# Four plain column tiles instead of three, the norm's matmul inside the first up product, and mixing chunk by chunk, in a two-layer decoder trunk

## The chip, the core and the metric

The kernel runs on one core of a Trainium2 chip. A core has five engines with instruction queues of their own, each worked off in order: TensorE (PE; its weight loads are listed as PEld), VectorE (DVE), ScalarE (ACT), GpSimd (POOL) and SyncE (SP), the last of which issues most DMA transfers here. The metric is the device time of one execution in microseconds, as the median of several.

## What is computed

Sixteen learned meta tokens stand ahead of 512 real ones, so L = 528; the model width is D = 1024. Two pre-norm residual layers follow, each a token mixer and a SwiGLU feed-forward (D_FF = 2816), and a last RMSNorm. Everything is float32.

```python
def rmsnorm(x, g):
    y = xf * lax.rsqrt(jnp.mean(xf * xf, axis=-1, keepdims=True) + EPS)
    return y * g
def swiglu(h, w_gate, w_up, w_down):
    return (jax.nn.silu(h @ w_gate) * (h @ w_up)) @ w_down

h = concatenate([meta, x])                       # (528, 1024)
h = h + pool_mixer(rmsnorm(h, g0), pool_w, pool_scale)   # layer 0: means over 2, 4, 8, 16 tokens, then 256x256 mixing by group
h = h + swiglu(rmsnorm(h, f0), gate0, up0, down0)
h = h + sb_mixer(rmsnorm(h, g1), w_qkv, w_o)             # layer 1: stick-breaking attention, 16 heads
h = h + swiglu(rmsnorm(h, f1), gate1, up1, down1)
return rmsnorm(h, final_norm)[16:]
```

## The kernel before

The residual stream is held transposed, in eight chunks `h` of 128 channels by 528 tokens (`hT[c]`). A float32 product is done as three fp32r products of a high and a low part (`mm3`, L106: high by high, high by low, low by high). The high part of a weight is a cast on ACT (L92, names that end in h), the low part a subtraction on DVE (L97, names that end in l). Raw weights arrive by DMA on SP's queue in six buffers; the split parts have eight buffers each for high and low.

**Layer 0's start.** The pool mixer writes pooled chunks into PSUM and then mixes them: sixteen tiles `mix` of 128 by 264, one for each chunk c and each token half hf, halves outside and chunks inside. DVE adds each to `h` (L266). When both halves of a chunk are done, `norm.chunk(c)` prepares it for the feed-forward: ACT scales it by the norm's gains and rounds it (`f0uh`, L152), DVE forms the rest (`f0ul`, L153), ACT squares it and DVE sums the squares over the chunks (`f0sq`, L161; the last by `add_eps`, L128). The reciprocal root of the mean (`rstd`) isn't needed for these: the products take the unscaled chunks, and the result is scaled on the way out. The matmul by `ones` (L173, output `fb0p`; `fb1p` in layer 1) sums over the partitions and spreads the sum to all of them, and `rstd_of` makes `fb0r` of it: a table function on ACT (L135) and one Newton step on DVE (L136 to L139). PSUM has eight banks: in the mixing all eight are a pool of their own, so the first feed-forward tile gets a bank when the last mix tile has been read.

**The feed-forward** works on 22 column tiles of 128 of D_FF, in six rounds (`ROUNDS`: 2, then 4 each). The first `PLAIN` tiles are plain products: gate, then up, each over eight chunks (`pp`, in two pieces of 264 tokens in layer 0 and in one of 512 in layer 1). The others are done by Strassen's scheme with seven products (`pa`, `pb`, `pc`) instead of eight. These need `operands()`: normed chunks `xn` (which need `fb0r`), their sums `t` and high and low parts `xh`, `xl` (L381, L387, L389, L390) in four sets, and sums `s` of the weights (L400) with splits `ws_0` to `ws_6`. The down products of a round (`pd`; L304 adds them to `h`, layer 1 has them transposed back, L325 and L331) are spread through the next round.

**What sets the order.** The program is written in dependence order; a scheduler with estimated durations sets the order of the instructions on each engine ahead of the run, and the engine keeps to it. `tc.issue_after(ins)` holds the instructions written inside it behind `ins` on the same engine, without a wait. Layer 1 has the same scheme behind the attention, whose output product `pw` DVE adds to `h` (L660) in chunks of 128 by 512.

## Time and profile before

| | |
|---|---|
| median of 3 runs | 1059.41 us (1058.34 to 1059.82) |
| the profiled execution | 1062.8 us |
| its span | 1061.0 us |
| mean granted clock of TensorE | 0.985 |
| busy: PE, PEld, DVE | 1023.1, 949.3, 856.6 us |
| busy: ACT, POOL | 556.9, 6.2 us |
| read from HBM, written | 92.43 MB, 2.10 MB |
| chain that ended last | PE 78%, DVE 17% |

A row of the timeline has the start, the duration, the engine, the line, the operation, output<-inputs by the program's names (buffer numbers left out), the shapes and the count of rows joined; in brackets how long the engine was idle before it, and what ended that. Matmuls overlap in the pipeline, so from start to start tells more than a row's duration; DVE instructions overlap by some 0.08 us as well. A list of waits has the total, the number of times and the longest. A slice of the timeline has its bounds, then busy time and count of each engine, the clock granted to TensorE (1.00 is full), the DMA share and GB/s.

### The profile page before, as it was taken

The numbers are of one execution on the slowest core, as the hardware profiler recorded it, in microseconds if no ns is written. First come the engines' busy times: TensorE is split into PE (matmuls) and PEld (weight loads), VectorE is DVE, ScalarE is ACT, GpSimd is POOL, SyncE is SP. The second block draws the span as 40 slices with busy tenths as digits, with TensorE's granted clock in tenths as the row PEclk, the third lists the DMA queues.
The fourth block names the chain that finished last, engine by engine and source line by source line (L and its number), as shares of the span: only waits on it lengthen the run. The fifth ranks groups of instructions, "written<-read, shape, count | busy, mean of one in ns | idle before, by whom it ended". The sixth has DMA issues, their size and how long they took to land.

```text
span 1061.0 us, 18586 instructions
## 1 busy us (share of the span) xinstructions
PE 1023.1 (96%) x7302; PEld 949.3 (89%) x7302; DVE 856.6 (81%) x1529; ACT 556.9 (52%) x1131; POOL 6.2 (1%) x16
## 2 busy tenths in 40 slices
PE   8998999999999999999999998989999999999997
PEld 6997999999999998998888886867899999999985
DVE  7899987888878777678888987779977877788755
ACT  7555645454444455455555454555655444455544
POOL 1000000000000010000000000000000000000000
PEclk9999999999999999999999998989999999999999
DMA  9212323333333332211111211211223223333302
GB/s 351 72 51 69 128 94 100 101 100 100 100 100 100 99 120 82 78 40 61 40 51 37 69 58 66 80 62 58 100 100 115 84 100 99 100 100 120 109 31 80
DMA packets 43112, 95.73 MB, mean 90 GB/s; under 512 B 3328, under 2 KB 20096, under 8 KB 43024
## 3 DMA queue, kind: packets, MB, share of 16 engines
q1 hardware_dynamic: 42272, 93.40, 26.2%
q8 instruction: 57, 0.93, 0.3%
q10 hardware_dynamic: 752, 1.14, 0.3%
q14 instruction: 31, 0.25, 0.1%
HBM read 92.43 MB, written 2.10 MB: 89 GB/s over the span
## 4 chain that ended last, share of the span: by engine, by line
PE 78%; DVE 17%; issue 2%; ACT 1%; DMA 1%; SPq 0%; ACTq 0%; DVEq 0%
PE pb L106 15%; PE pd L106 11%; PE pd L331 11%; PE pa L106 10%; PE pc L106 10%; PE pj L106 9%; PE pp L106 4%; DVE kp L581 2%; PE pw L106 2%; PE z L567 2%; DVE xl L390 1%; DVE a L619 1%; PE t L594 1%; DVE t L387 1%; DVE sg L583 1%
## 5 line engine op out<-in xcount | busy, mean ns | idle before, releaser
L304 DVE TENSOR_TENSOR h<-pd,h 128x264 f32<-128x264 f32 x96 | 40.9, 427 | 14.0 <-PE pd L106 14.0
L92 ACT CAST ws_3h<-rgate 128x512 fp32r<-128x512 f32 x38 | 23.6, 620 | 53.3 <-PE pb L106 47.8
L581 DVE TENSOR_TENSOR_SCAN kp<-kp,estrip 128x1344 f32<-128x1344 f32 x16 | 47.3, 2954 | 3.8 <-ACT kp L576 3.4
L92 ACT CAST ws_4h<-s 128x512 fp32r<-128x512 f32 x38 | 23.6, 621 | 46.6 <-PE pa L106 27.7
L92 ACT CAST ws_5h<-s 128x512 fp32r<-128x512 f32 x38 | 23.6, 621 | 45.8 <-PE pb L106 34.7
L433 DVE TENSOR_TENSOR u<-pb,m 128x264 f32<-128x264 f32 (+1 forms) x38 | 16.3, 428 | 38.6 <-PE pb L106 38.6
L106 PE MATMUL pa<-xl,ws_0h 128*128 128x264 f32 (+1 forms) x152 | 43.3, 285 | 3.1 <-DVE xl L390 3.0
L106 PE MATMUL pb<-xl,ws_1h 128*128 128x264 f32 (+1 forms) x152 | 43.3, 285 | 1.0 <-DVE xl L390 1.0
L106 PE MATMUL pc<-xl,ws_2h 128*128 128x264 f32 (+1 forms) x152 | 43.1, 283 | 0.9 <-DVE xl L390 0.9
L106 PE MATMUL pb<-xh,ws_1h 128*128 128x264 f32 (+1 forms) x152 | 43.6, 287 | 0.2 <-ACT xh L389 0.2
L106 PE MATMUL pa<-xh,ws_3h 128*128 128x264 f32 (+1 forms) x152 | 43.6, 287 | 0.0
L106 PE MATMUL pa<-xl,ws_3h 128*128 128x264 f32 (+1 forms) x152 | 43.5, 286 | 0.0
L106 PE MATMUL pa<-xh,ws_3l 128*128 128x264 f32 (+1 forms) x152 | 43.3, 285 | 0.0
L106 PE MATMUL pc<-xh,ws_2l 128*128 128x264 f32 (+1 forms) x152 | 43.2, 284 | 0.0
L106 PE MATMUL pa<-xh,ws_0h 128*128 128x264 f32 (+1 forms) x152 | 43.1, 284 | 0.0
L106 PE MATMUL pb<-xh,ws_6l 128*128 128x264 f32 (+1 forms) x152 | 43.0, 283 | 0.0
L106 PE MATMUL pa<-xh,ws_0l 128*128 128x264 f32 (+1 forms) x152 | 43.0, 283 | 0.0
L106 PE MATMUL pb<-xh,ws_4l 128*128 128x264 f32 (+1 forms) x152 | 43.0, 283 | 0.0
L106 PE MATMUL pc<-xl,ws_5h 128*128 128x264 f32 (+1 forms) x152 | 42.9, 283 | 0.0
L106 PE MATMUL pb<-xh,ws_1l 128*128 128x264 f32 (+1 forms) x152 | 42.9, 283 | 0.0
L106 PE MATMUL pb<-xl,ws_4h 128*128 128x264 f32 (+1 forms) x152 | 42.9, 282 | 0.0
L106 PE MATMUL pc<-xh,ws_5h 128*128 128x264 f32 (+1 forms) x152 | 42.9, 282 | 0.0
(1179 smaller groups left out, 4110.9 us busy)
## 6 DMA issues: line engine op xcount, KB each, us to landing
rgate<-in_ffn_w_gate_dram SPq DMA_DIRECT2D x44, 512.0 KB, 3.5
rup<-in_ffn_w_up_dram SPq DMA_DIRECT2D x44, 512.0 KB, 3.5
rd<-in_ffn_w_down_dram SPq DMA_DIRECT2D x42, 512.0 KB, 3.6
rq<-in_sb_w_qkv_dram SPq DMA_DIRECT2D x8, 512.0 KB, 3.5
rk<-in_sb_w_qkv_dram SPq DMA_DIRECT2D x8, 512.0 KB, 3.4
rv<-in_sb_w_qkv_dram SPq DMA_DIRECT2D x8, 512.0 KB, 3.4
rwo<-in_sb_w_o_dram SPq DMA_DIRECT2D x8, 384.0 KB, 3.0
h<-in_x_t_dram SPq DMA_DIRECT2D x8, 264.0 KB, 6.9
```

The source lines that it names most:

```text
L92: nc.scalar.copy(hi, v[:, j:j + w])
L106: last = nc.tensor.matmul(o, lhsT=w, rhs=xx[:, sl], start=start and i == 0, stop=stop and i == 2, skip_group_check=more)
L304: nc.vector.tensor_tensor(out=hv, in0=pd, in1=hv, op=ALU.add)
L331: nc.tensor.matmul(pd, lhsT=hid[j][x_][:, ts], rhs=w_[:, sl], start=r > 0 and i + j == 0, stop=j == len(hid) - 1 and i == 2, skip_group_ch ...
L387: nc.vector.tensor_tensor(out=o, in0=a, in1=b, op=ALU.subtract)
L390: nc.vector.tensor_tensor(out=xl[i][:, m, :], in0=o, in1=f32(xh[i][:, m, :]), op=ALU.subtract)
L433: tt(out=u[:, a], in0=pb, in1=m1, op=ALU.add)
L567: nc.tensor.matmul(tz[:, hd, c:c + k1 - k0], lhsT=qq[hs, i * P:(i + 1) * P], rhs=kk[hs, k0:k1], start=j == 0 and c == 0, stop=False, skip_ ...
L581: nc.vector.tensor_tensor_scan(kp[:, hd, ::-1], kp[:, hd, ::-1], estrip[:, ::-1], 1.0, op0=ALU.mult, op1=ALU.max)
L583: return nc.vector.tensor_tensor(out=sg[:, hd, 0:STRIP - 1], in0=sg[:, hd, 0:STRIP - 1], in1=kp[:, hd, 1:STRIP], op=ALU.mult).ins
L594: nc.tensor.transpose(o, sg[:, c0:c0 + n], ident)
L619: nc.vector.scalar_tensor_tensor(a0[r, i], f32(a0h[r]), lo_rows[r], p2[r, 256:384], op0=ALU.mult, op1=ALU.add)
```

## The change

Six edits go together. (1) `PLAIN` is 4: tile 3 becomes plain in both layers. (2) The mixing runs over chunks outside and halves inside, so that a chunk is complete, and its `norm.chunk` can begin, after every second mix tile. (3) The weight splits of a plain tile behind the first are held back on their engine: in layer 0 those of tiles 1 and 2, in layer 1 those of tile 1, behind `add_eps`'s instruction (`norm.done`); the later ones behind the last instruction of `rstd`. The hold acts on DVE, where both instructions run. (4) The norm's matmul stands inside tile 0's up product, right behind the one for chunk `FB` = 4, and the rest of the product behind it; the up product is held behind the gate product. (5) Gate and up results are read out of PSUM after both products are written. (6) `add_eps` and `norm_bcast` hand on their instructions for this.

```diff
-PLAIN = 3
+PLAIN = 4
+FB = 4
...
             if c == KC - 1:
-                add_eps(self.acc, sq, self.acc)
+                self.done = add_eps(self.acc, sq, self.acc)
...
-                nc.tensor.matmul(p, lhsT=ones, rhs=acc[:, o:o + h], start=i == 0, stop=i == len(accs) - 1)
+                last_bcast[:] = [nc.tensor.matmul(p, lhsT=ones, rhs=acc[:, o:o + h], start=i == 0,
+                                                  stop=i == len(accs) - 1).ins]
...
-        for hf in range(2):
-            for c in range(KC):
+        for c in range(KC):
+            for hf in range(2):
...
             def plain(f):
-                parts = [wsplit(raw_gu(kind, f), f"w{kind}{f}") for kind in ("gate", "up")]
+                parts = []
+                for kind in ("gate", "up"):
+                    with tc.issue_after(norm.done if f <= 2 - layer else fst[1]) if f else nullcontext():
+                        parts.append(wsplit(raw_gu(kind, f), f"w{kind}{f}"))
                 g, sg, u = (gw(f"{i}{f}") for i in ("g", "sg", "u"))
-                for dst, (wh, wl) in zip((g, u), parts):
+                prods = []
+                for i, (dst, (wh, wl)) in enumerate(zip((g, u), parts)):
                     pts = [ps(f"pp{f}", "w")[:, :sl.stop - sl.start] for sl in pieces]
+                    prods.append((dst, pts))
+                    mark = last if i and not fst else None
                     for k in range(KC):
-                        mm3([(t, slice(t0 + sl.start, t0 + sl.stop)) for t, sl in zip(pts, pieces)], wh[k], wl[k],
-                            uh[k], ul[k], k == 0, k == KC - 1)
-                    if not fst:
-                        fst.extend((norm_bcast([acc], f"fb{layer}", "d"), last_rstd[0]))
+                        with tc.issue_after(mark) if mark else nullcontext():
+                            last = mm3([(t, slice(t0 + sl.start, t0 + sl.stop)) for t, sl in zip(pts, pieces)], wh[k],
+                                       wl[k], uh[k], ul[k], k == 0, k == KC - 1)
+                        if i == 1 and k == FB and not fst:
+                            with tc.issue_after(last):
+                                fst.extend((norm_bcast([acc], f"fb{layer}", "d"), last_rstd[0]))
+                            mark = last_bcast[0]
+                for dst, pts in prods:
                     for t, sl in zip(pts, pieces):
```

How the edits move instructions is shown at three places; the numbers in the names tell buffers apart. Lines of the changed kernel are two to thirteen higher than those of the same statement before. First, DVE in layer 0 around the last residual add of the mixing, before:

```order
L97 TENSOR_TENSOR wgate1l_816<-rgate_1_813,wgate1h_815 128x512
L266 SCALAR_TENSOR_TENSOR h_71<-mix_497,gains,h_71 128x264
L97 TENSOR_TENSOR wgate1l_820<-rgate_1_813,wgate1h_819 128x512
L266 SCALAR_TENSOR_TENSOR h_72<-mix_512,gains,h_72 128x264
L161 TENSOR_TENSOR f0sq_435<-f0sq_435,f0sq_449 128x528
L266 SCALAR_TENSOR_TENSOR h_73<-mix_527,gains,h_73 128x264
L153 SCALAR_TENSOR_TENSOR f0ul_461<-h_68,gains,f0uh_460 128x528
L97 TENSOR_TENSOR wup1l_826<-rup_1_823,wup1h_825 128x512
L97 TENSOR_TENSOR wup1l_830<-rup_1_823,wup1h_829 128x512
```

and now:

```order
L269 SCALAR_TENSOR_TENSOR h_71<-mix_481,gains,h_71 128x264
L155 SCALAR_TENSOR_TENSOR f0ul_421<-h_68,gains,f0uh_420 128x528
L269 SCALAR_TENSOR_TENSOR h_72<-mix_496,gains,h_72 128x264
L163 TENSOR_TENSOR f0sq_379<-f0sq_379,f0sq_424 128x528
L155 SCALAR_TENSOR_TENSOR f0ul_444<-h_69,gains,f0uh_443 128x528
L269 SCALAR_TENSOR_TENSOR h_72<-mix_504,gains,h_72 128x264
L269 SCALAR_TENSOR_TENSOR h_73<-mix_519,gains,h_73 128x264
L269 SCALAR_TENSOR_TENSOR h_73<-mix_527,gains,h_73 128x264
```

Tile 1's splits are gone from around the last add, and four f0ul stand ahead of it instead of two. The splits follow after `add_eps`, ahead of the norm's Newton step:

```order
L130 SCALAR_TENSOR_TENSOR f0sq_379<-f0sq_539,f0sq_379 128x528
L99 TENSOR_TENSOR wgate1l_816<-rgate_1_813,wgate1h_815 128x512
L99 TENSOR_TENSOR wgate1l_820<-rgate_1_813,wgate1h_819 128x512
L99 TENSOR_TENSOR wup1l_826<-rup_1_823,wup1h_825 128x512
L99 TENSOR_TENSOR wup1l_830<-rup_1_823,wup1h_829 128x512
L99 TENSOR_TENSOR wgate2l_949<-rgate_2_946,wgate2h_948 128x512
L99 TENSOR_TENSOR wgate2l_953<-rgate_2_946,wgate2h_952 128x512
L99 TENSOR_TENSOR wup2l_959<-rup_2_956,wup2h_958 128x512
L138 TENSOR_TENSOR fb0t<-fb0r 128x528
```

Second, DVE in layer 1 around the last residual add of the attention (`h_73<-pw_7`), before:

```order
L660 TENSOR_TENSOR h_72<-pw_6_8506,h_72 128x512
L153 SCALAR_TENSOR_TENSOR f1ul_8448<-h_69,gains,f1uh_8447 128x528
L97 TENSOR_TENSOR wup1l_8778<-rup_1_8775,wup1h_8777 128x512
L161 TENSOR_TENSOR f1sq_8384<-f1sq_8384,f1sq_8429 128x528
L153 SCALAR_TENSOR_TENSOR f1ul_8472<-h_70,gains,f1uh_8471 128x528
L660 TENSOR_TENSOR h_73<-pw_7_8528,h_73 128x512
L97 TENSOR_TENSOR wup1l_8782<-rup_1_8775,wup1h_8781 128x512
```

and now:

```order
L673 TENSOR_TENSOR h_72<-pw_6_8489,h_72 128x512
L155 SCALAR_TENSOR_TENSOR f1ul_8431<-h_69,gains,f1uh_8430 128x528
L163 TENSOR_TENSOR f1sq_8367<-f1sq_8367,f1sq_8412 128x528
L155 SCALAR_TENSOR_TENSOR f1ul_8455<-h_70,gains,f1uh_8454 128x528
L673 TENSOR_TENSOR h_73<-pw_7_8511,h_73 128x512
```

Three of tile 1's four splits stood ahead of the last add; now none does. Third, PE in layer 0 where tile 3 begins, behind the first down products, before:

```order
L106 MATMUL pd_0_1093<-hl_706,wd_0_0h_1081 128x264
L106 MATMUL pd_0_1093<-hh_705,wd_0_0l_1082 128x264
L106 MATMUL pd_0_1093<-hh_942,wd_0_0h_1081 128x264
L106 MATMUL pa_1161<-xh_550,ws_0h_1133 128x264
L106 MATMUL pa_1161<-xl_557,ws_0h_1133 128x264
```

and now:

```order
L108 MATMUL pd_0_1093<-hl_706,wd_0_0h_1081 128x264
L108 MATMUL pd_0_1093<-hh_705,wd_0_0l_1082 128x264
L108 MATMUL pd_0_1093<-hh_942,wd_0_0h_1081 128x264
L108 MATMUL pp_1144<-f0uh_375,wgate3h_1123 128x264
L108 MATMUL pp_1145<-f0uh_375,wgate3h_1123 128x264
```

The first matmul that needs a Strassen operand (`xh`, `xl`) stood at row 543 of PE's program and stands at row 655 now. Over the whole program PE has 7096 rows instead of 7120, DVE 1461 instead of 1479, ACT 1064 instead of 1080; SP's and POOL's queues hold the same instructions in the same order.

## The prediction

> **What bounds the kernel now.** I read the page first, for the bound of the whole.

> ```profile
> PE 1023.1 (96%) x7302; PEld 949.3 (89%) x7302; DVE 856.6 (81%) x1529; ACT 556.9 (52%) x1131; POOL 6.2 (1%) x16
> PE 78%; DVE 17%; issue 2%; ACT 1%; DMA 1%; SPq 0%; ACTq 0%; DVEq 0%
> ```

> PE is busy for 96% of the span, so a change has two ways to gain: fewer matmuls, or fewer holes and half-clock stretches on PE. DVE's 17% of the chain that ended last says where the holes come from. Next I asked what PE waits for.

> ```profile
> PE pp L106 <- DVE h L660: 4.1, 1, 4.1
> ...
> PE pa L106 <- DVE xl L390: 3.0, 3, 2.1
> ```

> These are a first plain matmul behind the attention's last residual add (L660), and Strassen products behind their low operands (L390). Then I went through the stretches around the two feed-forwards; the columns are PE, PEld, DVE, ACT and POOL busy with counts, the granted clock, DMA share and GB/s.

> ```profile
> 35.00:40.00 5.00, 2.81 (x20) 2.63 (x19) 5.00 (x10) 4.96 (x10) 0.00 (x0) 0.89 0.28 97
> 40.00:45.00 5.00, 5.00 (x35) 5.00 (x34) 5.00 (x9) 4.02 (x7) 0.00 (x0) 0.77 0.20 66
> ...
> 80.00:85.00 5.00, 2.42 (x16) 1.93 (x15) 5.00 (x11) 2.23 (x7) 0.00 (x0) 1.00 0.27 92
> 85.00:90.00 5.00, 3.98 (x18) 3.58 (x18) 5.00 (x14) 2.07 (x7) 0.00 (x0) 0.66 0.03 13
> 90.00:95.00 5.00, 4.16 (x24) 3.15 (x23) 5.00 (x15) 3.04 (x10) 0.00 (x0) 0.99 0.16 52
> 95.00:100.00 5.00, 5.00 (x41) 4.91 (x41) 5.00 (x12) 3.19 (x9) 0.00 (x0) 1.00 0.01 3
> ```

> ```profile
> 695.00:700.00 5.00, 4.84 (x12) 3.85 (x13) 4.93 (x9) 1.38 (x2) 0.00 (x0) 0.50 0.30 105
> 700.00:705.00 5.00, 5.00 (x21) 4.05 (x20) 1.69 (x3) 0.98 (x2) 0.00 (x0) 0.90 0.00 0
> ...
> 735.00:740.00 5.00, 3.95 (x27) 3.36 (x25) 5.00 (x11) 1.76 (x5) 0.00 (x0) 1.00 0.00 0
> 740.00:745.00 5.00, 4.53 (x27) 3.95 (x28) 5.00 (x13) 3.29 (x9) 0.00 (x0) 1.00 0.01 3
> 745.00:750.00 5.00, 3.94 (x22) 3.08 (x21) 5.00 (x14) 4.63 (x12) 0.00 (x0) 0.88 0.11 34
> 750.00:755.00 5.00, 5.00 (x36) 5.00 (x36) 4.46 (x9) 2.52 (x6) 0.00 (x0) 0.78 0.51 173
> ```

> PE loses time at four places: A, the start of layer 0's feed-forward (35 to 42); B, its first Strassen products (80 to 95), where DVE is full in every slice; C, the start of layer 1's (691 to 701); D, its first Strassen products (735 to 752), DVE full again until 750. In A and C PE waits once and then runs at half clock; in B and D it starves for operands, and drops to half clock too.

> **Part A: mixing chunk by chunk, tile 1's splits behind the norm.**

> ```profile
> 35.26 0.28 PE L106 MATMUL mix<-ph,pw0h 128*128 128x264 f32 x1
> ...
> 36.59 0.28 PE L106 MATMUL mix<-ph,pw1l 128*128 128x264 f32 x1
> 39.06 0.78 PE L106 MATMUL pp<-f0uh,wgate0h 128*128 128x264 f32 x2 [2.19 <-DVE h L266]
> ```

> ```profile
> 36.81 0.68 DVE L97 TENSOR_TENSOR wgate1l<-rgate,wgate1h 128x512 fp32r<-128x512 f32 x1
> ...
> 38.43 0.49 DVE L266 SCALAR_TENSOR_TENSOR h<-mix,gains,h 128x264 f32<-128x264 f32 x1
> 38.83 0.76 DVE L153 SCALAR_TENSOR_TENSOR f0ul<-h,gains,f0uh 128x528 fp32r<-128x528 f32 x1
> 39.51 1.29 DVE L97 TENSOR_TENSOR wup1l<-rup,wup1h 128x512 fp32r<-128x512 f32 x2
> ...
> 47.92 0.71 DVE L128 SCALAR_TENSOR_TENSOR f0sq<-f0sq,f0sq 128x528 f32<-128x528 f32 x1
> ...
> 54.96 0.70 DVE L139 SCALAR_TENSOR_TENSOR fb0r<-fb0t,fb0r 128x528 f32<-128x528 f32 x1
> ```

> Twelve matmuls of 264 columns start within 36.59 - 35.26 = 1.33 us, 0.121 each. The first plain product waits for the last residual add (its bank is the last mix tile's), which starts 0.40 us before the next instruction. The new order puts 16 adds in pairs and lets the norm's chunk work (f0ul 0.68, sums of squares about 0.62) fill the time in which DVE waits between mix tiles, and takes two tile-1 splits (0.60 to 0.65 each) from ahead of the last add. Adding those durations from the first mix tile on, the last add starts at about 37.9 instead of 38.43: PE starts 0.6 us earlier, after a hole of 1.6 us instead of 2.19. The sum of squares (L128) is done near 44.1 instead of 48.6, as four splits (2.5 us) and the late chunk work are gone from ahead of it.

> The holes of B, for comparison:

> ```profile
> 81.04 0.39 PE L106 MATMUL pb<-xl,ws_1h 128*128 128x264 f32 x1 [0.97 <-DVE xl L390]
> ...
> 85.60 0.39 PE L106 MATMUL pa<-xl,ws_0h 128*128 128x264 f32 x1 [2.15 <-DVE xl L390]
> ```

> Half clock costs (1 - 0.89) x 5 + (1 - 0.77) x 5 = 1.7 us by the slices, of which 1.5 is after the restart. Is it paid after 1.6 us too? Behind the hole of 0.97 the clock stayed full (the slice from 80 has 1.00), behind those of 2.15 (0.66 in the slice from 85) and 2.19 it did not. 1.6 stands in the middle of 0.97 and 2.17, so the rows leave it open; what tips it is that the slice from 735, with 1.05 us of idle in pieces, kept its full clock too, and that no other hole lies near A's. I take it as avoided (+1.5), bounds 0 and +1.7.

> [...]

> **The norm's matmul inside the first up product.** In before it starts after 90 of tile 0's 96 matmuls, at 51.42.

> ```profile
> 51.42 1.05 PE L173 MATMUL fb0p<-f0sq,ones 128*128 128x264 f32 x4
> ```

> Now it is tied behind 48 gate and 30 up matmuls: 38.5 + 78 x 0.121 = 47.9, later than the sum of squares (44.1), so PE does not wait for it. The chain from it to the end of fb0r took 55.6 - 51.4 = 4.2 us with one split (0.6) inside; the new order has none inside. So fb0r is done near 51.4: 4.2 us earlier. No cost on PE: two matmuls either way.

> **Part B: tile 3 plain, layer 0.** A plain tile is 2 x 8 x 3 x 2 = 96 matmuls, a Strassen tile 7 x 4 x 3 = 84: +12 x 0.121 = +1.5 us of PE. What B costs today:

> ```profile
> 77.45 0.28 PE L106 MATMUL pa<-xh,ws_0h 128*128 128x264 f32 x1
> ...
> 95.36 0.28 PE L106 MATMUL pa<-xl,ws_3h 128*128 128x264 f32 x1
> ```

> ```profile
> 97.20 1.11 DVE L390 TENSOR_TENSOR xl<-t,xh 128x264 fp32r<-128x264 f32 x3
> ```

> From the first Strassen matmul to the row at 95.36 are 77 matmuls: 77 x 0.121 = 9.3 us of work that took 17.9, so 8.6 lost; I use 8.5. The last operand is done at 98.3, 20.8 us behind the first Strassen matmul. In the new order 112 PE rows more stand ahead of that matmul (13.6 us), less the 2.1 of A and 0.4 at the norm's matmul: it moves to about 88.6. DVE has 99 instructions from fb0r to the last operand today, in 42.6 us (0.43 each, no idle); it will have 112: 51.4 + 48.2 = 99.6, and about 1.2 more because it now reaches tile 3's gate and up evacuations slightly before PE has finished them. So the last operand comes 11.0 to 12.2 us behind the first Strassen matmul instead of 20.8, a relief of 8.6 to 9.8 against 8.5 lost: just enough, and by matching row to row the closest pairs stand 0.6 us apart. I leave 0.6 lost (bounds 0 and 4). B: +8.5 - 0.6 - 1.5 = +6.4.

> What is queued behind these on DVE: tile 4's raw weights are needed at about 56.3, sooner after fb0r than tile 3's Strassen sums were; SP's and POOL's queues issue the same sequence.

> **Part C: layer 1's start.**

> ```profile
> 690.62 0.40 PE L106 MATMUL pw<-os7h,wo_7l 128*128 128x512 f32 x1
> 695.16 0.77 PE L106 MATMUL pp<-f1uh,wgate0h 128*128 128x512 f32 x1 [4.15 <-DVE h L660]
> ...
> 701.18 0.40 PE L106 MATMUL pp<-f1uh,wgate0l 128*128 128x512 f32 x1
> ...
> 704.91 0.40 PE L106 MATMUL pp<-f1uh,wup0h 128*128 128x512 f32 x1
> ...
> 705.60 0.61 PE L173 MATMUL fb1p<-f1sq,ones 128*128 128x264 f32 x2
> ```

> ```profile
> 710.31 0.71 DVE L139 SCALAR_TENSOR_TENSOR fb1r<-fb1t,fb1r 128x528 f32<-128x528 f32 x1
> ...
> 748.38 0.75 DVE L390 TENSOR_TENSOR xl<-t,xh 128x256 fp32r<-128x256 f32 x2
> ```

> Three tile-1 splits (0.60 each) leave DVE's queue ahead of the last add: PE starts 1.8 us earlier, at 693.3, after a hole of 2.4 instead of 4.15. That is above the 2.15 and 2.19 that throttled, so half clock comes again. Today it lasts from the restart to 701.1, 5.9 us at half speed (2.9 lost); from a hole shorter by 1.8 I expect one period as in A (3.4 us, 1.7 lost): +1.2, bounds 0 and +2.9. At full clock 16 matmuls of 512 columns take 704.91 - 701.18 = 3.73, 0.233 each. The norm's matmul moves from row 33 to row 39 of the tile, about 704.3; it waits for nothing (the sum of squares is done near 699), and fb1r is done near 708.6 against 711.0. Tile 2's four splits (2.4 us) now come behind it, which D's count includes. C: +1.8 + 1.2 = +3.0.

> **Part D: layer 1's Strassen start.** Here a tile is one piece: 48 x 0.233 = 11.2 us plain, 84 matmuls of 256 columns at 0.118 (0.121 scaled by columns) = 9.9 for Strassen: +1.2 us of PE.

> ```profile
> 734.98 0.28 PE L106 MATMUL pa<-xh,ws_0h 128*128 128x256 f32 x1
> ...
> 752.38 0.28 PE L106 MATMUL pa<-xh,ws_0l 128*128 128x256 f32 x1
> ```

> Between these rows stand 52 matmuls of 256 columns, 16 of 512 and 16 transposes (a group of four about 0.44): 6.1 + 3.7 + 1.8 = 11.6 us of work in 17.4, so 5.8 lost. The last operand is done at 749.1, 14.1 us behind the first Strassen matmul; the 82 DVE instructions from fb1r took 38.1 (0.465 each). Now 95 of them: 708.6 + 44.2 = 752.8, while the first Strassen matmul moves to about 743.5: 9.3 behind. A relief of 4.8 against 5.8 lost; I leave 1.0 lost (bounds 0 and 3.5). D: +5.8 - 1.0 - 1.2 = +3.6.

> **Sum**: A 0.6 + 1.5, B 6.4, C 3.0, D 3.6 = 15.1 us. Everything between is PE without holes, so the gains add. The profiled execution took 1062.8 us (span 1061.0), 0.3% above the median of 1059.41: 1062.8 - 15.1 = 1047.7 on its own time, 1044.3 on the median; a part of the clock's terms may be smaller in executions that are faster already, so I say **1044.5**.

> **Rivals.** (1) *DVE stays the bound, and the wait moves to tile 4.* For it: DVE is full in B and D; three evacuations now stand in its queue ahead of operands and wait for PE; relief and loss are nearly equal. Against: the row-by-row distances stay positive. Then half of B and D's loss remains (7.1 less, clock periods with it): a gain of 7 to 9, 1050 to 1052.5. (2) *Slower.* The same loop closing: DVE waits at tile 3's up evacuation (it needs PE's last up matmul, about 88.7), and the 25 instructions behind it up to the last operand (11 us) gate PE, which starves as today and throttles again. It decides when operands come 15 us later in both layers together than summed; then B and D lose 14.3 as before, the 2.7 of added PE work is bare, and the clock costs what it did in A and C: 1059.4 + 2.7 - 2.4 + about 3.4 for two more periods = 1063. (3) *The holes only move*: B loses as today, D half, and no clock is saved: 0.6 - 1.5 + 1.8 + 2.9 - 1.2 = 2.6 or less, 1057 to 1061. Two independent failures, so less likely than one of them. (4) *C's hole does not throttle*: if where a hole falls decides beside its length, one of 2.4 may pass: +1.7 over the forecast, 1042.8. [...]

> **How the numbers follow.** Forecast, with A's clock either way and residuals near those taken (1043.5 to 1048): 0.55. Rival 4 with small residuals (1040 to 1043.5): 0.13. Rival 1 (1048 to 1054): 0.23. Rival 3: 0.04. Rival 2: 0.05. Runs of this kernel scatter by 0.14%, so 0.2%, 2.1 us, is about what can be told from no change. Faster than 1057.3: 0.91; within: 0.04; slower: 0.05. The range 1040.5 to 1053 leaves out rivals 2 and 3 and the ends of 1 and 4.

> **What would show it.** A: the first pp of layer 0 waits 1.6 for h, and the slice behind it has the clock at 1.00. The norm's matmul at 48, and the last fb0r instruction ending near 51.4. B: PE without holes from 39 to past 105, first Strassen matmul near 88.6. C: a wait near 2.4 and a clock loss of 1.7. D: PE slices from 733 (in the new time, some 10 us earlier) at 4.8 or above. I am wrong if pa, pb or pc of tile 4 wait for xl by more than 2 us in either layer, if DVE idles before s or xl, waiting for raw weights, or if PE waits for the sum of squares at the norm's matmul.

## The result and the profile after

The changed kernel takes 1045.6 us (median of 4 runs, 1045.07 to 1047.39) against 1059.62; the ratio is 0.9865 (95% interval 0.9846 to 0.9883). Forecast were 1044.5 and a range of 1040.5 to 1053. Run again beside the later experiments it took 1045.16, ratio 0.9865 (0.9848 to 0.9881).

The page of the changed kernel's profiled execution (1047.39 us, the slowest of the four; span 1045.6), first the busy times, then the chain that ended last:

```profile
PE 1017.1 (97%) x7278; PEld 943.5 (90%) x7278; DVE 846.4 (81%) x1511; ACT 550.8 (53%) x1115; POOL 6.2 (1%) x16
PE 84%; DVE 11%; issue 2%; ACT 1%; DMA 1%; SPq 0%; ACTq 0%; DVEq 0%
```

DVE's share of the chain fell from 17% to 11%. The list of what PE waits for (total, times, longest) has no operand `xl` and no `xh` left; the two holes at the feed-forwards' starts remain, shorter:

```profile
PE pp L108 <- DVE h L673: 2.3, 1, 2.3
PE pp L108 <- DVE h L269: 1.6, 1, 1.6
...
PE pc L108 <- ACT ws_2h L94: 0.3, 1, 0.3
```

The slices at the four places (PE, PEld, DVE, ACT, POOL busy, the granted clock, DMA share, GB/s), layer 0 first, with the pooling stage ahead of it:

```profile
20.00:25.00 5.00, 5.00 (x30) 5.00 (x31) 5.00 (x12) 4.61 (x11) 0.00 (x0) 0.69 1.03 407
...
35.00:40.00 5.00, 3.38 (x28) 3.19 (x28) 5.00 (x11) 3.83 (x7) 0.00 (x0) 1.00 0.00 2
40.00:45.00 5.00, 4.99 (x41) 5.00 (x42) 4.96 (x8) 3.62 (x7) 0.00 (x0) 1.00 0.02 3
...
90.00:95.00 5.00, 5.00 (x44) 5.00 (x43) 5.00 (x13) 2.72 (x6) 0.00 (x0) 1.00 0.26 99
95.00:100.00 5.00, 5.00 (x40) 4.67 (x39) 5.00 (x14) 3.48 (x9) 0.00 (x0) 1.00 0.32 105
100.00:105.00 5.00, 4.66 (x38) 4.44 (x37) 5.00 (x12) 3.10 (x8) 0.00 (x0) 1.00 0.35 108
```

```profile
680.00:685.00 5.00, 2.65 (x12) 1.85 (x11) 5.00 (x9) 4.41 (x8) 0.00 (x0) 1.00 0.20 80
685.00:690.00 5.00, 5.00 (x16) 3.90 (x16) 4.85 (x8) 2.64 (x5) 0.00 (x0) 0.66 0.00 0
...
735.00:740.00 5.00, 5.00 (x31) 4.29 (x30) 5.00 (x12) 3.17 (x7) 0.00 (x0) 1.00 0.15 62
740.00:745.00 5.00, 5.00 (x40) 4.68 (x39) 4.83 (x11) 2.66 (x7) 0.00 (x0) 1.00 0.35 107
745.00:750.00 5.00, 4.83 (x32) 4.05 (x31) 2.95 (x6) 3.49 (x10) 0.00 (x0) 1.00 0.29 105
```

B and D are nearly full of matmuls now; DVE is as full as before at B, and at D until 740. A runs at full clock behind its hole; C still pays one stretch at half clock. New is half clock in the pooling stage: its holes (0.93 and 0.68 us) and the order of PE, DVE and ACT up to there are those of before, but here the holes were followed by it, and the mixing ended 1.5 us later. The timeline of PE at the predicted points:

```profile
38.10 0.28 PE L108 MATMUL mix<-ph,pw1l 128*128 128x264 f32 x1
40.02 0.48 PE L108 MATMUL pp<-f0uh,wgate0h 128*128 128x264 f32 x2 [1.63 <-DVE h L269]
...
49.59 1.05 PE L175 MATMUL fb0p<-f0sq,ones 128*128 128x264 f32 x4
...
90.58 0.28 PE L108 MATMUL pa<-xh,ws_0h 128*128 128x264 f32 x1
...
684.87 0.47 PE L108 MATMUL pp<-f1uh,wgate0h 128*128 128x512 f32 x1 [2.35 <-DVE h L673]
...
735.56 0.28 PE L108 MATMUL pa<-xh,ws_0h 128*128 128x256 f32 x1
```

and of DVE, the norm's last instruction and the last operand of layer 0:

```profile
52.65 0.71 DVE L141 SCALAR_TENSOR_TENSOR fb0r<-fb0t,fb0r 128x528 f32<-128x528 f32 x1
...
102.10 0.42 DVE L403 TENSOR_TENSOR xl<-t,xh 128x264 fp32r<-128x264 f32 x1
```

### The profile page after: what moved, and what is told of

Its sections match the earlier page's. It is cut to its first block, busy times and chain, and to the rows that moved or that the text cites. A ratio compares the mean times of both kernels' runs of the same rounds, so it can differ in the third digit from the quotient of the medians.

```text
span 1045.6 us, 18479 instructions
## 1 busy us (share of the span) xinstructions
PE 1017.1 (97%) x7278; PEld 943.5 (90%) x7278; DVE 846.4 (81%) x1511; ACT 550.8 (53%) x1115; POOL 6.2 (1%) x16
## 4 chain that ended last, share of the span: by engine, by line
PE 84%; DVE 11%; issue 2%; ACT 1%; DMA 1%; SPq 0%; ACTq 0%; DVEq 0%
PE pb L108 15%; PE pd L108 12%; PE pd L334 12%; PE pa L108 10%; PE pc L108 10%; PE pp L108 9%; PE pj L108 9%; DVE kp L594 2%; PE pw L108 2%; PE z L580 2%; DVE a L632 1%; PE t L607 1%; DVE sg L596 1%; PE mix L108 1%; DVE h L673 1%
## 5 line engine op out<-in xcount | busy, mean ns | idle before, releaser
L446 DVE TENSOR_TENSOR u<-pb,m 128x264 f32<-128x264 f32 (+1 forms) x36 | 15.4, 427 | 35.6 <-PE pb L108 35.5
L108 PE MATMUL pc<-xh,ws_2h 128*128 128x264 f32 (+1 forms) x144 | 40.7, 282 | 0.3 <-ACT ws_2h L94 0.3
L108 PE MATMUL pa<-xh,ws_0h 128*128 128x264 f32 (+1 forms) x144 | 40.8, 283 | 0.0
L108 PE MATMUL pb<-xh,ws_1h 128*128 128x264 f32 (+1 forms) x144 | 40.8, 283 | 0.0
L108 PE MATMUL pb<-xh,ws_6l 128*128 128x264 f32 (+1 forms) x144 | 40.7, 283 | 0.0
L108 PE MATMUL pc<-xh,ws_2l 128*128 128x264 f32 (+1 forms) x144 | 40.7, 283 | 0.0
L108 PE MATMUL pb<-xl,ws_1h 128*128 128x264 f32 (+1 forms) x144 | 40.7, 283 | 0.0
L108 PE MATMUL pa<-xl,ws_3h 128*128 128x264 f32 (+1 forms) x144 | 40.7, 283 | 0.0
L108 PE MATMUL pa<-xh,ws_3h 128*128 128x264 f32 (+1 forms) x144 | 40.7, 283 | 0.0
L108 PE MATMUL pb<-xl,ws_6h 128*128 128x264 f32 (+1 forms) x144 | 40.7, 282 | 0.0
L108 PE MATMUL pa<-xl,ws_0h 128*128 128x264 f32 (+1 forms) x144 | 40.6, 282 | 0.0
```

The source lines that it names most:

```text
L108: last = nc.tensor.matmul(o, lhsT=w, rhs=xx[:, sl], start=start and i == 0, stop=stop and i == 2, skip_group_check=more)
L446: tt(out=u[:, a], in0=pb, in1=m1, op=ALU.add)
```

## The experiments

Below, "lost" is time in which PE did no matmul at its usual pitch: from the start of one PE row to that of another, less the matmuls between them at 0.1217 us (264 columns), 0.1185 (256), 0.2315 (512) and 0.09 (a transpose, as the mean of a group of four). At B and D it is taken over the 40 us behind the first Strassen matmul, and is good to about 0.1 us. A stretch at half clock costs 1.7 us by the slices in every trace, and is named apart. By this count the kernel before lost 6.8 us and one stretch at B, 4.4 and one stretch at D; the changed kernel 1.1 at B and 1.2 at D, without one.

**The fourth plain tile alone** (`x_plain4`), on the kernel before:

```diff
-PLAIN = 3
+PLAIN = 4
```

> The kernel before with PLAIN = 4 as its only edit. My theory (operand supply against demand): the last operand comes 112 DVE instructions after fb0r, about 103.8, and the first Strassen matmul moves 13.6 us down to about 91, so 12.8 us lie between them instead of 20.8: a relief of 8.0 of the 8.5 us lost at layer 0's first Strassen products; in layer 1 5.5 of 5.8. Less 1.5 and 1.2 us of added matmuls: a gain of about 10.5 us against before, 1049, with the holes and the half clock at the start of both feed-forwards as before. Rival (the earlier norm is what matters, the fourth plain tile only adds work): no gain or up to 2.7 us slower.

Measured: 1053.31 us, ratio 0.9932 (0.991 to 0.9953), a gain of 6.6 us against 10.5 expected. Layer 1's place went as expected (0.5 lost). Layer 0's didn't: 2.0 lost and a stretch at half clock. Its waits, in the timeline of PE, are for ACT, whose `xh` and `hh` casts follow DVE's results:

```profile
97.68 0.36 PE L106 MATMUL pd<-hh,wd_4h 128*128 128x264 f32 x1 [1.01 <-ACT hh L349]
98.71 0.39 PE L106 MATMUL pb<-xh,ws_1h 128*128 128x264 f32 x1 [0.55 <-ACT xh L389]
```

At A its hole is that of before, and the clock behind it is full, as PE's timeline and the slice show:

```profile
39.24 0.48 PE L106 MATMUL pp<-f0uh,wgate0h 128*128 128x264 f32 x2 [2.19 <-DVE h L266]
```

```profile
40.00:45.00 5.00, 5.00 (x43) 5.00 (x43) 5.00 (x9) 4.72 (x9) 0.00 (x0) 1.00 0.24 79
```

So the fourth tile gives nearly half of the 14 us by itself, and the rival (it only adds work) is out; but without the earlier norm layer 0 is short of operands by some 2 us. The profile is of the fastest of its four runs; the two slowest took 3.1 us more, at a granted clock of 0.988 against 0.992, and no trace shows where.

**Everything but the fourth plain tile** (`x_rest`), on the changed kernel:

```diff
-PLAIN = 4
+PLAIN = 3
```

> The changed kernel with PLAIN = 3: all edits but the fourth plain tile. My theory: 0.6 and 1.5 (clock) at layer 0's start, 1.8 and 1.2 at layer 1's, and about 1 us of relief at the Strassen products, since fb0r and PE's arrival both move earlier: a gain of about 6 us, 1053.5; DVE operands still leave PE waiting some 7 us in layer 0 and 5 in layer 1. Rival (the earlier norm does it): a gain of 12 or more, 1047, with these waits gone.

Measured: 1058.04 us, ratio 0.9981 (0.9968 to 0.9995): a gain of 2, not of 6. The holes at A and C are the changed kernel's to 0.01 us (1.63 and 2.35), but the Strassen products lost more than in the kernel before: 7.2 us at B (6.8 before), and 5.3 with a stretch at half clock at D (4.4 before). B's waits in the timeline of PE:

```profile
81.47 0.39 PE L108 MATMUL pd<-hh,wd_1h 128*128 128x264 f32 x1 [1.47 <-DVE h L307]
85.11 0.39 PE L108 MATMUL pb<-xh,ws_1h 128*128 128x264 f32 x1 [1.53 <-ACT xh L402]
...
87.34 0.39 PE L108 MATMUL pd<-hh,wd_2h 128*128 128x264 f32 x1 [0.79 <-DVE h L307]
90.75 0.39 PE L108 MATMUL pa<-xl,ws_0h 128*128 128x264 f32 x1 [1.43 <-DVE xl L403]
```

Half clock left out, PE reaches B 0.4 us sooner after the mixing than before and loses 0.4 more there; it reaches D 1.6 sooner after the attention and loses 0.9 more. The two halves of the change gain 6.6 and 2 alone and 14 together, which fits this reading: the early start pays only when the place behind it isn't bound by DVE.

**Halves outside, chunks inside again** (`x_nomix`):

```diff
-        for c in range(KC):
-            for hf in range(2):
+        for hf in range(2):
+            for c in range(KC):
```

> The changed kernel with the mixing over halves outside and chunks inside, as before. My theory: the last residual add comes about 0.7 us earlier than in the changed kernel (hole about 0.9), but six of eight chunks' f0ul and squares are left for after it, 1.3 us of DVE per chunk against 0.73 us of PE: tile 0's gate product waits for f0ul, about 2.5 us in all, and its clock may fall: 1 to 3.5 us slower than the changed kernel, 1046.5 to 1049. Rival (chunk order is indifferent, the holds do it): the same as the changed kernel, 1045.6, within 1.

Measured: 1048.98 us, ratio 0.989 (0.9867 to 0.9912), 3.4 slower than the changed kernel. The hole shrank to 0.99, and the gate product then waited for f0ul, three rows of this kind, 1.8 us lost up to the norm's matmul:

```profile
39.34 0.49 PE L108 MATMUL pp<-f0uh,wgate0h 128*128 128x264 f32 x2 [0.99 <-DVE h L269]
43.82 0.51 PE L108 MATMUL pp<-f0ul,wgate0h 128*128 128x264 f32 x2 [0.30 <-DVE f0ul L155]
```

The mechanism is as expected: the order of the mixing is worth its place because the norm's chunk work is spread under it. By size the trace shows 1.1 us of it, by which the norm's matmul comes later behind the last mix matmul (12.6 against 11.5). The profile is of the slowest of the four runs and has three half-clock stretches in the attention, where the changed kernel has two; so how much of the 3.4 belongs to the order stays open.

**No hold on the splits** (`x_nohold`):

```diff
-                    with tc.issue_after(norm.done if f <= 2 - layer else fst[1]) if f else nullcontext():
+                    if True:
```

> The changed kernel without holding the plain tiles' weight splits on DVE. My theory: the splits stand ahead of the last residual adds again; layer 0's hole 0.6 to 1.2 us longer (near 2.2 to 2.8, so half clock again, 1.5), layer 1's 1.8 longer (near 4.1, nearly 6 us of half clock): 3.5 to 6 us slower than the changed kernel, 1049 to 1051.5; the Strassen products as in the changed kernel. Rival (the holds only move splits to where they delay the norm's result): the same or up to 1 us faster.

Measured: 1051.16 us, ratio 0.9915 (0.9894 to 0.9935), 5.6 slower than the changed kernel, inside the expectation. The holes in its timeline, A and C:

```profile
40.78 0.48 PE L108 MATMUL pp<-f0uh,wgate0h 128*128 128x264 f32 x2 [2.50 <-ACT f0sq L159]
...
688.30 0.56 PE L108 MATMUL pp<-f1uh,wgate0h 128*128 128x512 f32 x1 [4.15 <-DVE h L673]
```

They grew by 0.9 and 1.8 us. (The first row names ACT's square, which ended at 40.68; the last residual add ended at 40.63.) B lost 1.1 us as in the changed kernel, D 0.5. The rest of the 5.6 can't be read from its one profile, which is the fastest of its four runs and has A at full clock behind 2.50; its runs at 1052 have a mean granted clock of 0.988 against 0.991.

**The norm's matmul placed by the scheduler** (`x_fbfree`):

```diff
-                    mark = last if i and not fst else None
+                    mark = None
...
-                        if i == 1 and k == FB and not fst:
-                            with tc.issue_after(last):
-                                fst.extend((norm_bcast([acc], f"fb{layer}", "d"), last_rstd[0]))
-                            mark = last_bcast[0]
+                    if not fst:
+                        fst.extend((norm_bcast([acc], f"fb{layer}", "d"), last_rstd[0]))
```

> The changed kernel with the norm's matmul placed by the scheduler, as before (in layer 0 it then stands 21 rows earlier on PE, in layer 1 five rows later), and gate and up products free to mix. My theory: what counts is when fb is ready against the first Strassen matmul, and that has only 0.6 to 1 us of slack missing: layer 0's remaining loss of about 1.2 us falls by up to 1, layer 1's is unchanged or 0.5 more: 1044.5 to 1046. Rival (the fixed place is worth its keep): 2 us or more slower than the changed kernel.

Measured: 1046.35 us, ratio 0.9874 (0.9858 to 0.989). That is 0.35 past the expectation's end and no difference that can be told: B lost 0.7 instead of 1.1, fb0r being ready 1.6 us earlier. No part of the gain can be seen to come from the fixed place of the norm's matmul in this order.

**A fifth plain tile** (`x_plain5`):

```diff
-PLAIN = 4
+PLAIN = 5
```

> The changed kernel with PLAIN = 5. My theory: the loss at the first Strassen products is nearly gone (1.2 us in layer 0 and 0.9 in layer 1), so a fifth plain tile adds 1.5 + 1.2 us of matmuls and can win back at most that loss: 0.5 to 2.7 us slower than the changed kernel, 1046 to 1048.5. Rival (DVE is still the bound behind tile 4): faster, 1042 or less.

Measured: 1048.54 us, ratio 0.9893 (0.9878 to 0.9909), 2.9 slower than the changed kernel, just past the expectation's end: nothing is lost at B (0.0) and 0.5 at D, and 2.7 us of matmuls came on top. Four is the number at which the loss has nearly gone.

**One PSUM pool at A** (`x_bankA`), held from the pooling to the end of layer 0's feed-forward; `turn()` hands out six banks "w" and two "d" in turn, so that the first feed-forward tile doesn't wait for the last mix tile:

```diff
-    with tc.tile_pool(name="start", bufs=1) as sp, phase("ps0", one=8):
+    banks = phase("ps1", w=6, d=2)
+    banks.__enter__()
+    with tc.tile_pool(name="start", bufs=1) as sp:
...
-                pm = ps(f"mix{c}{hf}", "one")[:, :HALF]
+                pm = ps(f"mix{c}{hf}", turn())[:, :HALF]
```

> The changed kernel with one PSUM pool for the mixing and layer 0's feed-forward, so that the first feed-forward tile takes a bank that was read eight tiles earlier instead of waiting for the last mix tile. My theory: the hole of 1.63 us in front of the first feed-forward matmul shrinks to 0.3 or less and all that follows moves up, the norm's matmul too: 1.3 to 1.6 us faster than the changed kernel, 1044, and half clock never at this place. Rival (the hole is not the bank but the chunks: PE would wait for f0ul instead, or the gain is given back at the first Strassen products): the same as the changed kernel.

Measured: 1046.42 us, ratio 0.9875 (0.9856 to 0.9894): the rival's time. The hole went (from the last mix matmul to the first gate matmul 0.12 us instead of 1.92), but the mixing itself took 0.7 longer, the order put twelve more down products ahead of the first Strassen matmul (which stands 52.5 us behind the last mix matmul in both kernels), and B lost 2.1 us instead of 1.1, and a stretch at half clock behind this row of its timeline:

```profile
96.26 0.39 PE L108 MATMUL pb<-xh,ws_1h 128*128 128x264 f32 x1 [1.62 <-ACT xh L410]
```

**One pool at A and at C** (`x_bankAC`); for C the attention's one-bank tiles are two tags of two, and layer 1's products take the attention's banks:

```diff
-    with tc.tile_pool(name="att", bufs=1) as ap, phase("ps2", one=4, two=2):
+    ctx.enter_context(phase("ps2", oa=2, ob=2, two=2))
+    with tc.tile_pool(name="att", bufs=1) as ap:
...
-                pa, pb, pc = [ps(f"p{i}{f}", "w")[:, :n] for i in "abc"]
+                    pab = ps(f"pab{f}", "two", 2)
+                    pa, pb, pc = pab[:, 0, :n], pab[:, 1, :n], ps(f"pc{f}", "oa")[:, :n]
```

> As the kernel with one PSUM pool for mixing and layer 0's feed-forward, and also one pool for the attention and layer 1's feed-forward. My theory: the hole of 2.35 us in front of layer 1's first feed-forward matmul goes too, and with it the 3.4 us at half clock (1.6 lost); some 0.6 us of waiting for the last chunk's f1ul remains: 4.5 to 5.5 us faster than the changed kernel, 1040.5. Rival (given back at the first Strassen products, where DVE is full): 1043 to 1045.

Measured: 1049.59 us, ratio 0.9905 (0.9887 to 0.9923), slower than the changed kernel by 4. The hole and the half clock at C went, but the edit changed the order within the attention, which took 288.2 us instead of 279.8; what a clean removal of C's hole by the bank is worth stays open.

The next four ran on one chip, the changed kernel among them.

**The changed kernel again** (`x_again`).

> The changed kernel once more, as the measure for the three others on the same chip: 1045.6, 14 us below before. In its profile I expect the hole of 1.6 us in layer 0 and of 2.35 us in layer 1 to the hundredth, and the stretches at half clock to be others in number or place than in the first profile (4 of them: one in the pooling, two in the attention, one behind layer 1's hole), since they have so far come and gone with equal holes.

Measured: 1045.16 us. Holes of 1.62 and 2.31; C ran at full clock this time, and the attention had one half-clock stretch instead of two. Its slices for the pooling and for C:

```profile
20.00:25.00 5.00, 5.00 (x31) 5.00 (x30) 5.00 (x13) 4.60 (x11) 0.00 (x0) 0.66 1.03 406
...
685.00:690.00 5.00, 5.00 (x23) 4.11 (x22) 4.85 (x8) 2.24 (x5) 0.00 (x0) 1.00 0.00 0
```

**One pool at A and the norm's matmul behind chunk 2** (`x_bankA_fb2`):

```diff
-                        if i == 1 and k == FB and not fst:
+                        if i == 1 and k == (2 if full else FB) and not fst:
```

> One PSUM pool for mixing and layer 0's feed-forward as in the earlier run, where the hole went but was given back at the first Strassen products, and the norm's matmul behind chunk 2 of the up product instead of chunk 4 in layer 0. My theory now: what is lost there follows the distance from the first Strassen matmul to the last operand (8.2 us apart lost 0.6, 11.7 to 11.9 lost 1.1 to 2.0, 13.5 lost 2.0 and a half-clock stretch of 1.7); an earlier norm (fb0r 2 us earlier) brings it from 13.5 to about 11.5: about 1 us lost, no half clock there, so 1.5 to 2 us faster than the changed kernel, 1043.7. Rival (no supply in time however early the norm is, DVE's work alone decides): the loss stays 2 to 3.7, 1046.4 as before.

Measured: 1045.69 us, ratio 0.9869 (0.9854 to 0.9883). The expectation failed: counted from the last mix matmul, fb0r came 1.1 us earlier than in the changed kernel (14.1 against 15.2), but the first Strassen matmul came 1.4 earlier too (51.1 against 52.5; the twelve down products are behind it again). So the distance from it to the last operand was 13.2 instead of about 11.5, and 2.4 us were lost. Of the 1.8 us gained at A, 1.3 are handed back at B, and the slower mixing takes 0.7 and a wait in the gate product 0.3.

**Chunk work behind the last residual add at C** (`x_lateC`); `tail[0]` is that add, and f1ul and the sum of squares of a chunk are held behind it:

```diff
-        for c, st in enumerate(wo(5, NP)):
-            st()
-            norms[1].chunk(c)
+        for st in wo(5, NP):
+            st()
+        for c in range(KC):
+            norms[1].chunk(c, tail[0] if c >= 3 else None)
```

> The changed kernel with the f1ul and the sums of squares of chunks 3 to 7 held behind the attention's last residual add on DVE. My theory: three DVE instructions leave the queue ahead of that add (0.68 + 0.62 + 0.68), less what DVE must wait for the last product: the hole in front of layer 1's first feed-forward matmul falls from 2.35 to about 1.1 us, and with that half clock behind it is rarer: 1.2 to 2.9 us faster than the changed kernel, 1043.5. Rival (moved on): the sum of squares comes later and PE waits for it at the norm's matmul, or for f1ul inside the gate product: the same as the changed kernel.

Measured: 1043.9 us (1043.76 to 1045.53), ratio 0.9853 (0.9838 to 0.9867), 1.3 below the changed kernel beside it. The hole fell by 1.36 us, and a short wait for f1ul came in its place:

```profile
682.44 0.47 PE L108 MATMUL pp<-f1uh,wgate0h 128*128 128x512 f32 x1 [0.99 <-DVE h L679]
688.22 0.50 PE L108 MATMUL pp<-f1ul,wgate0h 128*128 128x512 f32 x1 [0.34 <-DVE f1ul L158]
```

About half of the early start was kept: the first Strassen matmul stands 51.2 us behind the attention's last product instead of 51.8 (`x_again`, full clock there too), and D lost 1.2 us in both. The two profiled executions differ by 1.1 us: 0.6 here and 1.3 in the pooling (one half-clock stretch fewer), less 0.8 in the attention (one more). It is the fastest of the versions by its median, though its interval overlaps that of the changed kernel.

**Both** (`x_combo`).

> Both of these edits together. My theory: the places are 640 us apart and share nothing, so the gains add: 3 to 4.5 us faster than the changed kernel, 1042. Rival: either edit's gain is lost at the Strassen products behind it, 1044 or more.

Measured: 1044.34 us, ratio 0.9855 (0.984 to 0.987). The rival: 0.4 more than the edit at C alone; at A 1.8 us gained, at B 1.3 lost, and 0.7 in a slower mixing.

## Why the prediction held, step by step

Profiled execution against profiled execution, 1061.0 to 1045.6 us of span, by the start times of PE's rows:

| step | predicted | measured |
|---|---|---|
| A, start | 0.6 | 2.47 to 1.92 us from the last mix to the first gate matmul: 0.55 |
| A, clock | 1.5 | 1.5 |
| B, with 12 more matmuls | 6.4 | 8.5 to 1.1 lost, less 1.5: 5.9 |
| C, start | 1.8 | 4.54 to 2.74: 1.80 |
| C, clock | 1.2 | two stretches to one, 2.8 to 1.7 lost: 1.1 |
| D, plain for Strassen | 3.6 | 6.1 to 1.2 lost, less 1.2: 3.7 |
| pooling | none | 1.5 later (a stretch at half clock) |
| attention | none | 281.8 to 279.8: 2.0 earlier (two stretches instead of three) |
| sum | 15.1 | 15.1; the spans differ by 15.4, the rest in pieces under 0.15 |

**Right.** The holes (1.6 and 2.4 predicted, 1.63 and 2.35 measured), the order's effect on them, the relief at B and D by moving the demand down, and the added matmuls. `x_plain5` shows the last two from the other side. Relative to the end of the mixing, fb0r ended at 15.2 us (14.8 predicted), and the first Strassen matmul stood at 52.5 (52.0).

**Mis-sized.** B's remaining loss, 0.6 forecast and 1.1 measured, and its two parts: by `x_plain4` the fourth tile alone leaves 2.0 and a half-clock stretch, not 0.5, and by `x_rest` the earlier norm alone relieves nothing. The step at fault is the comparison of two distances (first Strassen matmul to last operand, 20.8 to 11.0–12.2). The distance was right (11.9 measured), but not all that stands in it is relief: operands are needed one by one, and the down products' adds and ACT's casts wait in the same queues. Over eight traces of layer 0 the distance and the loss without clock go together, with a scatter of 1 us: 8.2 us lost 0.7 (`x_fbfree`), 11.7 and 11.9 lost 2.0 and 1.1 (`x_plain4`, changed), 13.2 and 13.5 lost 2.4 and 2.1 (`x_bankA_fb2`, `x_bankA`), 19.7 and 20.8 lost 7.2 and 6.8 (`x_rest`, before), and `x_plain5`, whose last operand is ready 9.2 us ahead of that matmul, lost nothing. In layer 1 the distance is no such guide: 9.3 was forecast and 11.5 measured, and `x_fbfree` and `x_lateC` stand at 14.1 like the kernel before, but lose 1.2 where that one lost 4.4. So D's term came out right (1.0 forecast, 1.2 measured) without the comparison behind it.

**Right by number, with half of the reason.** I held A's half clock to be avoided because its hole shortened from 2.19 to 1.63. `x_plain4` has the 2.19 hole of before and the full clock behind it, `x_nohold` 2.50 and the full clock. At C, holes of 2.30 to 2.35 were followed by a stretch in four of the eight traces that have them, among these the first profile of the changed kernel but not the second. So the length alone doesn't decide.

What goes with a stretch in these traces was counted after the runs, and no run was made to test it. In the kernel before, stretches at half clock last 3.413 us (from 38.86, 86.65, 424.57 and 748.84) or twice that (from 656.67 and 694.22). In each trace they start whole multiples of 3.413 us apart (here 14, 113, 181, 192 and 208 steps behind the first). So a trace can be cut into steps of that length, counted from its first stretch, and the work of PE in each be compared. Here are two steps around the hole of 2.19 at A, in the kernel before:

```profile
35.45:38.86 3.41, 1.42 (x12) 1.21 (x10) 3.41 (x8) 3.38 (x7) 0.00 (x0) 1.00 0.10 25
38.86:42.28 3.42, 3.22 (x15) 3.25 (x16) 3.42 (x7) 3.42 (x7) 0.00 (x0) 0.50 0.44 157
```

and in `x_plain4`:

```profile
34.98:38.39 3.41, 2.07 (x18) 1.86 (x16) 3.41 (x8) 3.37 (x7) 0.00 (x0) 1.00 0.01 2
38.39:41.80 3.41, 2.56 (x21) 2.59 (x22) 3.41 (x7) 3.41 (x7) 0.00 (x0) 1.00 0.49 159
```

In the first, 1.99 us of the hole lie in one step, which has 12 matmuls, the outer ones in part (0.37 of its length at their usual pitch), and the next step runs at half clock. In the second the hole is split, 1.34 and 0.85 us, over two steps with 18 and 21, and neither is followed by half clock. At the pooling, A, B, C and D of all fourteen traces, each of the 24 stretches that begin from full clock follows a step with at most 0.43 of its length in matmuls (each row at its usual pitch, and at most up to the next row), and each of the 581 steps at full clock that none follows has 0.45 or more. The hole of 1.63 lies in a single step in all six traces that have it, and leaves 0.46 there. So the shorter hole stayed clear of half clock, though by this count narrowly (0.46 against 0.43), and the reason given was right in this; the hole of 2.19 has half clock behind it in the kernel before, where it falls mostly into one step, and none in `x_plain4`, where two share it, so a part of what the sum calls A's and C's clock (at C a hole of 4.15 had one stretch or two, one of 2.3 none or one) belongs to the executions and not to the change. The two misses of the sum, pooling and attention, are stretches too (one more, one fewer), and cancelled; ten of the twelve traces of the changed kernel and its variants have the one in the pooling, and neither of the two with the order of before.

Over all these runs, the mean granted clock of the kernel before lay between 0.985 and 0.990, mostly at 0.987; that of the changed kernel between 0.991 and 0.995. At spans of 1058 and 1044, 1 - 0.987 and 1 - 0.994 are 13.8 and 6.3 us: about 7 of the 14 us are, by the clock, fewer half-clock stretches, those at B and D among them, which came from starved operands. The forecast had 6.1 us of this in its terms (1.5 at A, 1.2 at C, and 1.7 each inside what B and D lost).

## What to carry to other kernels

Where a later stage waits for another engine's products, compare when the first consumer arrives with when the last operand is ready before shortening anything ahead of it: time gained in front can be handed back there, and two edits that move supply and demand apart pay together what neither does alone. More work on the bound engine can be the right way to move the demand, up to the point where the loss is gone and not one tile further. Before a hole is called worth its half clock, look at several executions: here one of 2.19 us had half clock behind it in one trace and none in another, and those of 2.30 to 2.35 in four of eight.
